# A decoder layer on one core: the fourth blocks of queries and keys as one unit by tokens, and the last eight heads beside w_out

## The chip, the core and the metric

The kernel runs on one core of one Trainium2 chip. The metric is device time in microseconds of one execution of the whole program; the figure given for a kernel is the median of its runs. The engines are named as in the profile: PE (matmuls; its weight loads are listed apart as PEld), DVE (vector), ACT (scalar activations), POOL (GpSimd), and SP, which issues DMAs. PSUM, where matmuls accumulate, has eight banks of 128 x 512 floats.

## What is computed

One layer of a hybrid decoder, all in float32, for 256 tokens of width 2048. In the reference, cut to what matters here:

```python
proj = einsum('bsd,de->bse', rmsnorm(h), w_in)            # z | x,B,C | dt | q | k | v
...                                                        # SSD heads -> y_ssm (256 x 2048)
qh = q.reshape(b, s, 16, 128) * 128 ** -0.5                # 16 heads of 128
for window, dilation in ((128, 1), (512, 4), (2048, 16)):  # three dilated causal windows
    o, l = dilated_window_attention(qh, kh, vh, window, dilation)
y_att = sum of the three outputs, weighted by softmax over their lse
h = h + rmsnorm(concat([y_ssm, y_att]) @ w_out)
h = h + rmsnorm(relu(rmsnorm(h) @ w_up) ** 2 @ w_down)
```

With 256 tokens the three windows become one softmax with a count of how often each key is seen (`m0`, `m1` hold the logarithm of the count). Queries, keys and values have 2048 columns each, in four blocks of 512 columns; a block holds four heads.

## The kernel before

**Precision.** Each float32 operand is split into a high part (`hi`, by ACT, L147) and a rest (`lo`, by DVE, L148), and a product takes three matmuls (hi x hi, hi x lo, lo x hi) at the fast float32 rate. So each weight tile that arrives by DMA costs ACT and DVE one split each, into one of `BUFS = 5` pairs of `hi` and `lo` buffers of 128 x 1024 (two stacked tiles of 128 x 512: one k is 256 rows of the weight).

**Three ways to multiply.** *By features* (`gemm_features`, `products`, L485 and L488): the weight is the stationary operand and the activations stream, so the result has features on the partitions, which is what the scores of attention want. *By tokens* (`row_tile`, L331 to L333): the activations are stationary and 512 weight columns stream; the result has tokens on the partitions. *By seven* (`seven`, L418 to L420): for one k, two blocks of columns and both halves of the tokens, seven products in place of eight, after Strassen and Winograd. It needs sums of activations (`sums_of_acts`, L377 to L383, kept once made), sums of weights on DVE (L252), four pairs of split buffers a group, and the sum of two weight tiles that POOL makes in DRAM by an accumulating DMA (`next_pair`, L279 and L280, four groups ahead); SP then loads it (L156). Its products go to eight banks: four in `acc` and four in `more`, of which two are the small-tile banks (`psmall`, two in all).

**A unit** (`unit`, L451) does two blocks of columns by tokens. It goes through k in a given order, each k plainly (two `row_tiles`, one a block) or by seven; at the first group of seven it calls `drain`, and after the last one `combine` takes `more` away. The last k is always plain and ends the accumulators. `keys_by_tokens` is such a unit for one block of queries with one of keys; since its results have tokens on the partitions, `turned_heads` turns them on PE (L966) and ACT copies them out (L967). `two_values` is such a unit for two blocks of values.

**What runs beside.** Work that isn't a GEMM is written as generators in the queue `waiting`. After each row tile or pair of weight tiles `pump(n)` takes n steps, each time from the generator at the front, which then goes to the back; `drain` runs all to their end. `heads(...)` puts two lanes there, each with two heads at a time: a step of scores and softmax (L907, L908 on PE; L915 to L921 on DVE and ACT), one that turns the probabilities (L929, copies L933), and one that multiplies by the values (L938, L939) and splits the result into `att`, the activations of w_out. The first two steps take both small banks.

**The order around the change.** Blocks are counted from zero. Queries and keys 0 are made by features (`keys_too`), then come the units of queries and keys 1, values 0 and 1, and queries and keys 2. Then:

- queries 3 by features, with pumps (1, 1, 0, 2, 1, 2, 2, 2) for the turns of unit 2 and for heads 0 to 7 (two lanes, twelve steps);
- the values 2 and 3;
- keys 3 by features, with pumps (0, 0, 1, 1, 1, 1, 2, 2) for heads 8 to 11;
- the first `EARLY = 5` k of w_out, for two blocks of columns: ten row tiles (L1278 to L1281), one pump each, for heads 12 to 15.

Then the pools of the attention are closed, and their memory becomes that of `hp`, where w_out keeps, among others, the buffers for sums (`tmp`). w_out goes on with its order (L440): k 5 and 7 plainly, then 6, 9 and 8 by seven, and so on.

**Who orders.** The program's order is a priority, and the scheduler of the language places each engine's instructions at build time; the splits and the sums have a higher priority (`high_priority`), and `in_line` keeps the splits of a unit in a fixed order. Heads and turns are tied behind the last row tile by `issue_after(product[t].ins)`.

Of the kernel before, what the change touches and what calls it, by code (L numbers as in the profile page):

```python
# [10 lines left out]
F32 = mybir.dt.float32  # L11
# [5 lines left out]
P = 128  # L17
S = 256
D = 2048
NT = S // P  # L20
# [15 lines left out]
COL_Q = COL_DT + 32  # L36
COL_K = COL_Q + NH * DH
COL_V = COL_K + NH * DH
NB = 512
# [38 lines left out]
def hymba_layer(ctx: ExitStack, tc: tile.TileContext, x, norm_mix_pre, w_in, conv_w, conv_b, dt_bias, a_log,  # L78
# [53 lines left out]
    def bank():  # L132
        return pacc.tile([P, NB], F32, name="acc")
# [298 lines left out]

    plan("z", w_z, 0, (0, 2, 4, 6, 1, 3, 5), (1, 3))
    plan("z", w_z, 2, (0, 2, 1, 4, 3, 6, 5), (1, 3, 5))
    qk_blocks = [(COL_Q + hb * NB, COL_K + hb * NB) for hb in range(3)]
    plan("qk", w_in, qk_blocks[1], (0, 2, 1, 4, 3, 5, 6), QK_SEVENS)
    plan("v", w_v, 0, range(7), V_SEVENS)
    plan("qk", w_in, qk_blocks[2], (0, 2, 1, 3, 4, 5, 6), QK_SEVENS)
    plan("v", w_v, 2, (0, 2, 1, 3, 4, 5, 6), V_SEVENS)
    plan("out", w_out, 0, (5, 7, 6, 9, 8, 11, 10, 13, 12), (6, 8, 9, 10, 12))  # L440
    plan("out", w_out, 2, (0, 6, 1, 9, 2, 12, 4, 3, 8, 5, 10, 7), (6, 9, 12, 4, 8, 10, 7))
# [7 lines left out]
    plan(("down", 1), w_downs[1], 2, (0, 1, 3, 2, 6, 8, 4, 11, 13, 5, 9, 12), (3, 6, 8, 11, 13, 9, 12))  # L449

    def unit(src, n, order, last, acc, more, combine, lag=0, at_end=(None, None), first=True, ending=None,  # L451
             ready=None, halves=None):


        cols = blocks_of(n)
        sevens = [k for k, by_seven in order if by_seven]
        for i, (k, by_seven) in enumerate(order):
            if i + 1 < len(order) and order[i + 1][1]:
                sums_of_acts(order[i + 1][0])
            if by_seven:  # L460
                if k == sevens[0]:
                    drain()
                    if ready:
                        ready()
                seven(src, *cols, k, acc, more, k == sevens[0], k == sevens[-1])
            else:
                for b in range(2):
                    row_tiles(src, cols[b], [k], acc[b::2], room["acts"], first and i == 0, False,
                              fetch=fetch_next)
            if k == sevens[-1]:  # L470
                combine(more)
        for b in range(2):
            if b and ending:
                ended.append(ending(cols[b], last, acc))
            else:
                row_tiles(src, cols[b], last, acc[b::2], room["acts"], False, True, lag if b else 0, at_end[b],
                          fetch=fetch_last if b else fetch_next, halves=halves if b else None)
# [488 lines left out]
                nc.tensor.transpose(p[:, f * P:(f + 1) * P], r[:, f * P:(f + 1) * P], ident)  # L966
        nc.scalar.activation(dst[:, :, t * P:(t + 1) * P], p.rearrange("p (f s) -> p f s", f=4), AF.Copy)  # L967

    def keys_by_tokens(hb, last, acc, more):

        if hb == 1:
            rstq.append(mp.tile([P, NT], F32, name="rstq"))
# [1 line left out]
        rows, both = [], []  # L974

        def ready():
            rows[:] = [not_yet[1][:, t:t + NT] for t in (0, NT)]
            both.append(mp.tile([P, 4, S], F32, name="cT", bufs=5))
            both.append(mp.tile([P, 4, S], F32, name="cT", bufs=5) if hb == 1 else
# [2 lines left out]
        def end(b):  # L982
            def at_end(t, a):
# [6 lines left out]

        unit(w_in, qk_blocks[hb], orders["qk", qk_blocks[hb]], last, acc, more,
             lambda x: combine_new([[v[:, t] for t in range(NT)] for v in rows], x), 0, (end(0), end(1)),
             ready=ready)
        return both

    rstq = []
# [54 lines left out]
    ap_ = ExitStack()  # L1051
    ap = ap_.enter_context(tc.tile_pool(name="ap", bufs=2, side="right", reuse_waits="tile"))
    heads((0, *qk[0], vs[0]), (1, *qk[1], vs[1]))
    q3 = queries(COL_Q + 3 * NB, rbq, (1, 1, 0, 2, 1, 2, 2, 2))
    own_places([mp.tile([P, 4, S], F32, name="cT", bufs=5).rearrange("p (k f) s -> p k (f s)", k=KB) for _ in range(2)])
    vs += two_values(2, [bank() for _ in range(2 * NT)], [])
    heads((2, *qk[2], vs[2]))
    qk.append((q3, queries(COL_K + 3 * NB, rbc, (0, 0, 1, 1, 1, 1, 2, 2))))
    heads((3, *qk[3], vs[3]))
    del room["own"], room["sum"]  # L1060


# [214 lines left out]
    acc = [bank() for _ in range(2 * NT)]  # L1277
    for k in range(EARLY):  # L1278
        for b in range(2):
            row_tiles(w_out, b * NB, [k], acc[b::2], part, k == 0, False, pumps=1,  # L1280
                      fetch=fetch_next)  # L1281
    assert not waiting
    ap_.close()
# [273 lines left out]
```

## Time and profile before

| | |
|---|---|
| median of 3 runs | 1453.36 us |
| lowest and highest | 1452.56 and 1453.89 us |
| span of the profiled execution, from its first to its last instruction | 1451.4 us |
| median over that span | 1.96 us |
| PE busy | 1442.4 us, 99% |
| DVE busy | 1300.4 us, 90% |
| ACT busy | 947.1 us, 65% |
| granted clock of PE | 0.999 |
| queries 3, from 482.5 us | 30.85 us |
| values 2 and 3, from 513.35 us | 47.76 us |
| keys 3, from 561.11 us | 29.34 us |
| the ten early row tiles of w_out, from 590.45 us | 33.92 us |

The profile is of one execution; times are from the start of its span. The stages in the lower rows were marked by the first matmul of each in PE's order of time. A busy PE need not be at its peak: the duration of a matmul includes its latency, and consecutive ones overlap, so what a matmul costs is read from the distance between starts. A line number is that of the kernel; many instructions carry the line of a helper (L147 and L148 are all splits).

### The profile page before, as it was taken

The numbers are of one execution on the slowest core, as the hardware profiler recorded it, in microseconds if no ns is written. First come the engines' busy times: TensorE is split into PE (matmuls) and PEld (weight loads), VectorE is DVE, ScalarE is ACT, GpSimd is POOL, SyncE is SP. The second block draws the span as 40 slices with busy tenths as digits, with TensorE's granted clock in tenths as the row PEclk, the third lists the DMA queues.
The fourth block names the chain that finished last, engine by engine and source line by source line (L and its number), as shares of the span: only waits on it lengthen the run. The fifth ranks groups of instructions, "written<-read, shape, count | busy, mean of one in ns | idle before, by whom it ended". The sixth has DMA issues, their size and how long they took to land.

```text
span 1451.4 us, 20394 instructions
## 1 busy us (share of the span) xinstructions
PE 1442.4 (99%) x7042; PEld 1214.7 (84%) x7042; DVE 1300.4 (90%) x1881; ACT 947.1 (65%) x1351; POOL 162.3 (11%) x244
## 2 busy tenths in 40 slices
PE   9999999999999999999999999999999999999998
PEld 8888888888888888888888888888888888888886
DVE  7788888988999788689988999999889999999998
ACT  7577669665666666556657677656465776766664
POOL 0201110131111000010100011010111110101000
PEclk9999999999999999999999999999999999999999
DMA  8977656756898658588976798688888888788854
GB/s 267 272 219 222 189 175 187 239 170 195 231 253 248 196 127 244 173 270 257 280 225 217 210 311 240 203 221 251 249 255 279 255 245 247 210 293 265 248 179 160
DMA packets 172359, 332.97 MB, mean 229 GB/s; under 512 B 16048, under 2 KB 18976, under 8 KB 172256
## 3 DMA queue, kind: packets, MB, share of 16 engines
q1 hardware_dynamic: 144736, 272.37, 58.1%
q0 software_dynamic: 19648, 45.63, 15.7%
q10 hardware_dynamic: 7872, 13.68, 2.8%
q8 instruction: 55, 0.90, 0.3%
q14 instruction: 48, 0.39, 0.1%
HBM read 327.39 MB, written 49.84 MB: 260 GB/s over the span
## 4 chain that ended last, share of the span: by engine, by line
PE 76%; ACT 1%; DVE 1%; DMA 0%; issue 0%; ACTq 0%
PE acc L331 10%; PE acc L333 10%; PE acc L332 10%; PE acc L418 7%; PE acc L419 7%; PE acc L420 7%; PE acc L485 4%; PE ps L331 3%; PE ps L332 3%; PE ps L333 3%; PE ps L418 2%; PE ps L419 2%; PE ps L420 2%; PE acc L488 2%; PE acc L1463 1%; PE ps L938 0%
## 5 line engine op out<-in xcount | busy, mean ns | idle before, releaser
L148 DVE TENSOR_TENSOR lo<-raw,hi 128x1024 fp32r<-128x1024 f32 (+1 forms) x387 | 470.1, 1220 | 79.1 <-ACT hi L147 76.3
L147 ACT ACTIVATE hi<-raw 128x1024 fp32r<-128x1024 f32 (+1 forms) x387 | 404.2, 1050 | 204.2 <-PE acc L333 71.4
L485 PE MATMUL acc<-ua,hi 128*128 128x512 f32 x520 | 141.2, 401 | 0.1
L147 ACT ACTIVATE hi<-e 128x1024 fp32r<-128x1024 f32 x66 | 70.2, 1063 | 68.5 <-DVE e L252 62.7
L485 PEld LDWEIGHTS acc<-ua,hi 128*128 128x128 f32 x520 | 91.3, 189 | 14.2 <-ACT hi L147 0.2
L331 PE MATMUL acc<-hi,ua 128*128 128x512 f32 x228 | 90.6, 397 | 0.0
L332 PE MATMUL acc<-lo,ua 128*128 128x512 f32 x228 | 89.3, 392 | 0.0
L333 PE MATMUL acc<-hi,ua 128*128 128x512 f32 x228 | 89.2, 391 | 0.0
L331 PE MATMUL acc<-hi,sh 128*128 128x512 f32 x220 | 86.9, 395 | 0.0
L333 PE MATMUL acc<-hi,sl 128*128 128x512 f32 x220 | 85.8, 390 | 0.0
L332 PE MATMUL acc<-lo,sh 128*128 128x512 f32 x220 | 85.7, 390 | 0.0
L488 PEld LDWEIGHTS acc<-ua,lo 128*128 128x128 f32 x520 | 76.5, 190 | 8.9
L148 DVE TENSOR_TENSOR lo<-e,hi 128x1024 fp32r<-128x1024 f32 x66 | 80.5, 1220 | 0.0
L488 PE MATMUL acc<-ua,lo 128*128 128x256 f32 x520 | 78.8, 282 | 0.0
L419 PE MATMUL acc<-lo,ah 128*128 128x512 f32 x180 | 70.1, 390 | 0.0
L420 PE MATMUL acc<-hi,al 128*128 128x512 f32 x180 | 70.1, 390 | 0.0
L418 PE MATMUL acc<-hi,ah 128*128 128x512 f32 x180 | 70.1, 390 | 0.0
L485 PE MATMUL acc<-uc,hi 128*128 128x512 f32 x208 | 61.4, 405 | 0.0
L148 DVE TENSOR_TENSOR lo<-ha,hi 128x1024 fp32r<-128x1024 f32 x43 | 52.5, 1221 | 6.0 <-ACT hi L147 5.8
L147 ACT ACTIVATE hi<-ha 128x1024 fp32r<-128x1024 f32 x43 | 45.2, 1057 | 19.4 <-PE acc L333 12.4
L147 ACT ACTIVATE hi<-r 128x512 fp32r<-128x512 f32 x66 | 41.5, 629 | 20.8 <-PE acc L333 8.8
L418 PE MATMUL acc<-hi,ua 128*128 128x512 f32 x137 | 53.7, 392 | 0.0
(572 smaller groups left out, 3722.3 us busy)
## 6 DMA issues: line engine op xcount, KB each, us to landing
raw<-in_w_in_dram SPq DMA_DIRECT2D x154, 512.0 KB, 4.5
raw<-in_w_down_dram SPq DMA_DIRECT2D x69, 512.0 KB, 5.7
raw<-in_w_up_dram SPq DMA_DIRECT2D x65, 512.0 KB, 4.8
raw<-in_w_out_dram SPq DMA_DIRECT2D x38, 512.0 KB, 5.1
raw<-pair SPq DMA_DIRECT2D x57, 256.0 KB, 4.3
pair<-in_w_up_dram POOLq DMA_DIRECT2D x56, 256.0 KB, 5.4
pair<-in_w_down_dram POOLq DMA_DIRECT2D x52, 256.0 KB, 6.3
pair<-in_w_in_dram POOLq DMA_DIRECT2D x42, 256.0 KB, 5.5
```

The lines of the kernel that those rows point to most:

```text
L147: return (nc.scalar.activation(hi, src, AF.Copy), nc.vector.tensor_tensor(lo, src, hi.bitcast(F32), op=ALU.subtract))
L148: nc.vector.tensor_tensor(lo, src, hi.bitcast(F32), op=ALU.subtract))
L331: nc.tensor.matmul(dst[:, cs], a_h[:, r, ts], hi[:, j, cs], start=begin and j == 0, stop=False)
L332: nc.tensor.matmul(dst[:, cs], a_h[:, r, ts], lo[:, j, cs], start=False, stop=False)
L333: product[t] = nc.tensor.matmul(dst[:, cs], a_l[:, r, ts], hi[:, j, cs], start=False, stop=end and j == KB - 1)
L418: nc.tensor.matmul(dst, a_h, hi[:, j], start=own and first, stop=False)
L419: nc.tensor.matmul(dst, a_h, lo[:, j], start=False, stop=False)
L420: nc.tensor.matmul(dst, a_l, hi[:, j], start=False, stop=own and last)
L485: nc.tensor.matmul(acc[f], hi[:, j, f * P:(f + 1) * P], u(k0 + j), start=k0 + j == 0, stop=False, skip_group_check=True)
L488: nc.tensor.matmul(acc[f][:, 0], lo[:, j, f * P:(f + 1) * P], u(k0 + j)[:, 0], start=False, stop=k0 + j == NK - 1, skip_group_check=True)
L1463: nc.tensor.transpose(p[:, f * P:(f + 1) * P], r[:, f * P:(f + 1) * P], ident)
```

## The change

Queries 3 and keys 3 are no longer two GEMMs by features but one unit by tokens (`keys_by_tokens(3, ...)`), with the order of k (0, 2, 4, 1, 3, 5, 6, then 7) and three groups of seven, 3, 5 and 6 (the third unit has four). It stands where queries 3 stood, ahead of the values; its plain row tiles pump (2, 2, 1, 1, 1, 1, 2, 2) steps for the turns of unit 2 and heads 0 to 7, and what is left is drained at its first group of seven. Its results go to two `tk` buffers and, turned on PE beside the values' first row tiles, to two `cT` buffers. The values take the unit's `more` as accumulators and its accumulators as their `more`. Heads 8 to 15 are now one queue of two lanes with twelve steps, and all of it runs beside w_out's ten early row tiles, which pump one step for the first block of columns and, from the second k on, two for the second.

```diff
-    qk_blocks = [(COL_Q + hb * NB, COL_K + hb * NB) for hb in range(3)]
+    qk_blocks = [(COL_Q + hb * NB, COL_K + hb * NB) for hb in range(4)]
...
     plan("qk", w_in, qk_blocks[2], (0, 2, 1, 3, 4, 5, 6), QK_SEVENS)
+    plan("qk", w_in, qk_blocks[3], (0, 2, 4, 1, 3, 5, 6), (3, 5, 6))
     plan("v", w_v, 2, (0, 2, 1, 3, 4, 5, 6), V_SEVENS)
...
     def unit(src, n, order, last, acc, more, combine, lag=0, at_end=(None, None), first=True, ending=None,
-             ready=None, halves=None):
+             ready=None, halves=None, pumps=(1,)):
...
+        turns = 0
...
                     row_tiles(src, cols[b], [k], acc[b::2], room["acts"], first and i == 0, False,
-                              fetch=fetch_next)
+                              pumps=pumps[turns % len(pumps)], fetch=fetch_next)
+                    turns += 1
...
-    def keys_by_tokens(hb, last, acc, more):
+    def keys_by_tokens(hb, last, acc, more, pumps=(1,)):
...
         def ready():
+            if hb == 3:
+                rows[:] = [mp.tile([P, NT, NB], F32, name="tk", bufs=3) for _ in range(2)]
+                both.extend(mp.tile([P, 4, S], F32, name="cT", bufs=5) for _ in range(2))
+                more.extend(f() for f in (psmall, bank, psmall, bank))
+                return
...
-             ready=ready)
+             ready=ready, pumps=pumps)
...
     heads((0, *qk[0], vs[0]), (1, *qk[1], vs[1]))
-    q3 = queries(COL_Q + 3 * NB, rbq, (1, 1, 0, 2, 1, 2, 2, 2))
+    acc, more = [bank() for _ in range(2 * NT)], []
     own_places([mp.tile([P, 4, S], F32, name="cT", bufs=5).rearrange("p (k f) s -> p k (f s)", k=KB) for _ in range(2)])
-    vs += two_values(2, [bank() for _ in range(2 * NT)], [])
-    heads((2, *qk[2], vs[2]))
-    qk.append((q3, queries(COL_K + 3 * NB, rbc, (0, 0, 1, 1, 1, 1, 2, 2))))
-    heads((3, *qk[3], vs[3]))
+    qk.append(keys_by_tokens(3, (7,), acc, more, (2, 2, 1, 1, 1, 1, 2, 2)))
+    vs += two_values(2, more, acc)
+    heads((2, *qk[2], vs[2]), (3, *qk[3], vs[3]))
...
     for k in range(EARLY):
         for b in range(2):
-            row_tiles(w_out, b * NB, [k], acc[b::2], part, k == 0, False, pumps=1,
+            row_tiles(w_out, b * NB, [k], acc[b::2], part, k == 0, False, pumps=1 + (k > 0 and b),
                       fetch=fetch_next)
```

## The prediction

> **What bounds the kernel now.** I read the page first, then who waited for whom on PE, and then the stretch that the change rebuilds, by windows. From the page, and from the list of PE's waits over the whole span (total, times, longest, in us):
>
> ```profile
> span 1451.4 us, 20394 instructions
> PE 1442.4 (99%) x7042; PEld 1214.7 (84%) x7042; DVE 1300.4 (90%) x1881; ACT 947.1 (65%) x1351; POOL 162.3 (11%) x244
> PE ps L1408 <- ACT dg L1407: 1.4, 1, 1.4
> PE ps L810 <- ACT bn L816: 0.6, 1, 0.6
> ```
>
> PE is busy 99% of the span, and its waits of any length are in the warm-up, in the SSD part (L810) and at the end (L1408); none lies in attention. So time is PE's own work: a microsecond of matmuls taken away is one won, and the only loss can be a wait that PE doesn't have now. The stretch in question, by stage (columns: from:to, length, busy of PE, PEld, DVE, ACT, POOL with counts, clock, DMA share, GB/s): the unit of the third query and key blocks, then q3 (with heads 0 to 7), the values, k3 (with heads 8 to 11) and the first ten tiles of w_out (with heads 12 to 15):
>
> ```profile
> 441.70:482.50 40.80, 40.80 (x181) 33.80 (x180) 38.14 (x45) 26.36 (x29) 4.87 (x7) 1.00 0.76 213
> 482.50:513.35 30.85, 30.85 (x190) 27.22 (x188) 20.91 (x46) 19.75 (x40) 1.90 (x3) 1.00 0.71 204
> 513.35:561.11 47.76, 47.76 (x227) 39.82 (x226) 41.77 (x73) 27.97 (x46) 3.52 (x5) 1.00 0.63 170
> 561.11:590.45 29.34, 29.33 (x174) 25.78 (x173) 20.61 (x45) 20.08 (x39) 0.00 (x0) 1.00 0.66 209
> 590.45:624.37 33.92, 33.92 (x166) 28.48 (x165) 23.09 (x54) 19.28 (x36) 1.35 (x2) 1.00 0.66 218
> ```
>
> PE is busy throughout at clock 1.00. DVE has room in q3, k3 and w_out's tiles (68% to 70%) and little in a unit by tokens (38.14 of 40.80, 93%).
>
> **The parts, on PE.** Removed: q3 and k3 by features, eight pairs of 128-row weight tiles each. PE's order of time in k3 (start, duration):
>
> ```profile
> 563.89 1.99 PE L485 MATMUL acc<-ua,hi 128*128 128x512 f32 x8
> 565.71 1.11 PE L488 MATMUL acc<-ua,lo 128*128 128x256 f32 x8
> 566.67 2.00 PE L485 MATMUL acc<-ua,hi 128*128 128x512 f32 x8
> ```
>
> From one start to the next (durations overlap, since matmuls are pipelined) a pair takes 566.67 - 563.89 = 2.78 us. 16 pairs are 44.5 us. Added: a unit by tokens. The values show its two kinds of step:
>
> ```profile
> 540.71 0.39 PE L331 MATMUL acc<-hi,ua 128*128 128x512 f32 x1
> 546.15 0.39 PE L418 MATMUL ps<-hi,ub 128*128 128x512 f32 x1
> 555.67 0.39 PE L331 MATMUL acc<-hi,uc 128*128 128x512 f32 x1
> ```
>
> Plain: 24 matmuls from 540.71 to 546.15, 5.44 us for one k and both columns blocks, 2.72 a row tile. By seven: 42 matmuls from 546.15 to 555.67 are two groups, 4.76 each, so a group saves 0.68. Eight k with three groups cost 8 x 5.44 - 3 x 0.68 = 41.5 us. The row of 441.70 agrees: the same unit with four groups took 40.80 = 41.5 - 0.68.
>
> Added too: 16 transposes of L966, in four groups, because a unit by tokens leaves q and k with tokens on the partitions. One such group inside q3, and its durations over the whole kernel (min/median/max ns):
>
> ```profile
> 485.30 0.60 PE L966 MATMUL acc<-ident,al 128*128 128x128 f32 x4
> 485.66 2.11 PE L485 MATMUL acc<-ua,hi 128*128 128x512 f32 x8
> 488.55 0.60 PE L966 MATMUL ps<-ident,al 128*128 128x128 f32 x4
> L966 PE MATMUL acc<-ident,al x16: 270/272/273, 401.8 to 495.3; 128*128 128x128 f32 x16
> ```
>
> The four hold the stream for 0.36 us, and the pair behind them takes 488.55 - 485.66 = 2.89 instead of 2.78: 0.46 a group, 1.84 for four. Sum of the terms: -44.5 + 41.5 + 1.84 = **-1.2 us**.
>
> The trace's 272 ns is a latency, not a hold of PE. [...]
>
> The heads' matmuls are the same, at other places. Price in w_out's tiles: 33.92 - 10 x 2.72 = 6.72 us for two lanes (two heads each), 3.36 a lane. A second sum, by stages at that price: new unit 41.5 + 1.84 (transposes of the third blocks, which q3 had) + 4 x 3.36 = 56.8; values 40.8 + 1.84 = 42.6; ten tiles 27.2 + 4 x 3.36 = 40.6; together 140.0 against 30.85 + 47.76 + 29.34 + 33.92 = 141.87: **-1.8 us**. The two differ by what breaking into a feature stream costs beyond breaking into a token stream, which no row separates. I take -1.5 and keep -1.2 and -1.8.
>
> **Costed at nothing.** DVE in the new unit: from the 441.70 row, a group fewer saves three adds (L252, 0.69), one split of 1.22 and one of 0.69, 4.0 together, so 34.1; four lanes add some 3.7 each (softmax from 499.74 to 502.72, 3.0, and a split of 0.68; these rows stand below), so 48.9 of PE's 56.8 us, 86%: hidden behind PE on average. The values have 38.1 of 42.6. POOL and DMA: three more pairs of accumulating copies ahead of the values' and w_out's own (four groups ahead), and fewer SP loads of 512 KB whole. One unit with four groups has POOL at 4.87 of 40.80 and DMA at 0.76 and no PE wait; three groups in 56.8 us ask less. If a pair came late, one wait of a landing, some 5 us, would show. What ACT and DVE did at the ends of q3 and k3 (L508, L509, L949) goes; the unit's combine and ends (L427 to L431, L986, L987) are what the third unit has already.
>
> **What can turn into a wait: two places.** First, w_out. Its first group of seven needs sums of activations, which need buffers in memory that the last heads give back:
>
> ```profile
> 612.26 0.59 PE L938 MATMUL ps<-pT,tk 128*128 128x256 f32 x2
> 613.49 0.48 PE L331 MATMUL acc<-hi,sh 128*128 128x512 f32 x1
> 613.60 1.23 DVE L148 TENSOR_TENSOR lo<-raw,hi 128x1024 fp32r<-128x1024 f32 x1 [2.25 <-ACT hi L147]
> 614.74 0.68 DVE L377 TENSOR_TENSOR r<-sh,sl 128x512 f32<-128x512 f32 x1
> 615.35 0.68 DVE L148 TENSOR_TENSOR al<-ps,ah 128x512 fp32r<-128x512 f32 x1
> 615.95 0.41 DVE L378 TENSOR_TENSOR r<-r 128x256 f32<-128x256 f32 x1
> 616.88 0.28 DVE L379 TENSOR_TENSOR r<-r 128x128 f32<-128x128 f32 x1
> 617.41 0.29 DVE L380 TENSOR_TENSOR r<-r 128x128 f32<-128x128 f32 x1
> 634.18 0.69 DVE L252 TENSOR_TENSOR e<-raw 128x512 f32<-128x512 f32 x1
> 647.89 1.22 DVE L148 TENSOR_TENSOR lo<-uc,hi 128x1024 fp32r<-128x1024 f32 x1
> 649.89 0.39 PE L332 MATMUL acc<-lo,ah 128*128 128x512 f32 x1
> 622.00:635.40 13.40, 13.40 (x61) 11.09 (x60) 10.68 (x17) 7.39 (x9) 1.90 (x3) 1.00 0.93 304
> 635.40:640.00 4.60, 4.60 (x22) 3.82 (x21) 3.94 (x6) 3.48 (x4) 0.00 (x0) 1.00 0.67 143
> 650.00:666.00 16.00, 16.00 (x73) 13.24 (x72) 16.00 (x24) 10.19 (x12) 2.17 (x3) 1.00 0.89 255
> ```
>
> DVE idled 2.25 us and began the sums (L377) right after the last head's products, which ran from 612.26 to 613.49. From there it works up to the tile that PE reads at 649.89, whose split ended at 647.89 + 1.22 = 649.11: 0.8 us of lead, the least I found; from 650 on DVE is busy 16.00 of 16.00. Now the last head follows the sixth of ten tiles; with pumps of 1, 1, 1, 2, 1, 2, ... twelve steps end behind the ninth, 3 x 2.72 = 8.2 us later against PE. By then the five split buffers (BUFS) can be full, so DVE's splits aren't late; the sums are. What is left to do at that point grows by about 3.5 us: the sums of group 6 (0.68 + 0.41 + 0.28 + 0.29 and a split of 0.68: 2.4) and all but the split of those of group 9 (1.7), one split of heads (0.7), less one split done earlier (1.2). DVE's idle time from 622 to 640 is 18.0 - 10.68 - 3.94 = 3.4 us. 3.4 + 0.8 covers 3.5, with nothing over: on time costs 0, and each microsecond that the heads end later costs about one.
>
> Second, the new unit's first group of seven drains the lanes at once: four steps with no tile between them. A lane's step takes both small PSUM banks, so they go one by one. From the heads of q3 and, for the transposes, of the values:
>
> ```profile
> 498.26 0.39 PE L907 MATMUL ps<-cT 128*128 128x128 f32 x2
> 499.74 0.28 DVE L915 CUSTOM_DVE_ANT_0 sm<-ps,cst 128x128 f32<-128x128 f32 x1
> 500.85 0.08 DVE L915 DVE_READ_ACCUMULATOR2_ANT mx<- 128x1 f32 x1
> 502.17 0.55 DVE L921 TENSOR_SCALAR sm<-sm,den 128x128 f32<-128x128 f32 x2
> 525.03 0.82 PE L929 MATMUL ps<-ident,sm 128*128 128x128 f32 x6
> 507.48 0.84 ACT L933 ACTIVATE pT<-ps 128x384 f32<-128x384 f32 x2
> 510.05 0.60 ACT L147 ACTIVATE ah<-ps 128x512 fp32r<-128x512 f32 x1 [0.97 <-PE ps L939]
> ```
>
> Scores until the banks are read: 498.26 to 500.93, 2.7 us, twice; transposes 0.6 (six, their durations overlapping) and copies 0.84, twice; two products of 613.49 - 612.26 = 1.23; split 0.60 + 0.68: 12 us, of which PE works some 6 (scores 1.2, transposes 0.6 and products 1.2, each twice). The other 6 must be filled. Of a group's 21 matmuls 15 need no small bank (3.4 us), and five buffers let two groups run so far, 6.8 us: just filled, if the order on PE puts them there. I take 0.5 us for both places together, from 0 and the two prices below.
>
> **Sum.** -1.5 + 0.5 = -1.0 us: the span would be 1450.4. The median shown is 1453.36, 1.96 over this span, and I keep that difference: **1452.4 us**. A measurement of this kernel tells 0.2% (2.9 us) from no change, so this is no change.
>
> **Rivals.**
> (A) The forecast: from -1.8 with no wait to about +0.5. 66%.
> (B) Slower: the heads end later than behind the ninth tile, since the fourth steps of the two lanes now come in one pump, each wants both small banks, and only one tile (2.72) follows until the first lane's fifth. If they need two tiles more, DVE's lead is 5.4 us short and PE waits at the second and third groups of seven: -1.5 + 5.4 = +3.9, 1457.3. Slower than before from 1.5 us of lateness, by more than 0.2% from 4.4. For it: 0.8 us of lead. Against: tiles further on can go ahead of a waiting head. 13%.
> (C) Slower: nothing fills the drain in the new unit, and 6 us of wait stand between its fourth k and its first group: -1.5 + 6 = +4.5, 1457.9. For it: PE takes matmuls as they are ordered. Against: the values drain too, and their PE is busy 47.76 of 47.76, though only one step is left there. 10%. [...]
> (D) Faster: the steps that are pumped in twos save some six breaks of 0.24 us beside the -1.8: -3.2, 1450.2. The L966 rows show 0.11 a break behind transposes; I doubt more. 7%.
> (E) A transpose holds PE for its whole duration, 16 x 0.272 = 4.4 instead of 1.84: -1.2 + 2.5 = +1.3, 1454.7; no gain from the change. Against: starts 0.36 us apart for four. 4%.
>
> **Range and chances.** (A) and (E) lie within 0.2%, with a little of (A) on the fast side; most of (D) is faster; half of (B) and nearly all of (C) slower. Faster 0.08, within 0.76, slower 0.16. From 1450.2 (D) to 1457.3 (the middle of B); outside are (C), half of (B) and the end of (D), under 0.2. (A) alone: 1451.6 to 1453.9.
>
> **What would show it.** L485 and L488 lose 256 starts in attention and L966 has 48 records, not 32; the stretch from the third unit's end to w_out's eleventh tile is 140 us instead of 141.87; PE's waits name neither L418 nor L331 there. (B) is wrong if L377 starts soon after the ninth tile and no wait for DVE shows at w_out's groups; (C) if the first L418 of the new unit follows without idling. I am wrong if the stretch shrinks by over 3 us, or if a wait shows in stages that the change doesn't touch.

## The result and the profile after

The changed kernel takes **1460.36 us** (median of 4 runs, 1459.92 to 1463.94) against 1452.96 us of the kernel before beside it (1452.37 to 1453.89): a ratio of 1.0055, 95% interval 1.0043 to 1.0068. Two later series of five runs each gave 1461.76 (1.0057, 1.0045 to 1.0070) and 1460.70 us (1.0051, 1.0037 to 1.0065). So it is slower by some 8 us, where 1 us less was forecast, and 3.1 us outside the range.

Line numbers of the changed kernel are a little higher than before: scores L910 and L911 (before L907, L908), the reading of the scores on DVE L918 (L915), the turned probabilities L932 (L929), the products with the values L941 and L942, the turns L969 (L966), the ends of a unit of queries and keys L994, those of the values L1019 and L1020. L331 to L333, L418 to L420, L147, L148 and L161 have kept theirs.

The page of the changed kernel, span and PE:

```profile
span 1462.2 us, 20325 instructions
...
PE 1446.7 (99%) x6985; PEld 1213.3 (83%) x6985; DVE 1308.6 (89%) x1892; ACT 952.8 (65%) x1358; POOL 166.9 (11%) x250
```

The profiled execution (1463.94 us) is the slowest of the four; why it is slower than the others is settled below. Its span is 10.8 us longer than the one before, and PE is counted busy 4.3 us longer, so two fifths of the loss is not idle time. The list of PE's waits over the whole span (total, times, longest, in us) names what is new:

```profile
PE ps L910 <- DVE mx L918: 4.8, 1, 4.8
PE ps L332 <- DVE lo L148: 1.5, 1, 1.5
...
PE acc L418 <- ACT hi L147: 0.5, 1, 0.5
PE acc L419 <- DVE lo L148: 0.2, 1, 0.2
```

None of the four stands in the list before. By windows (from:to, length, busy of PE, PEld, DVE, ACT, POOL with counts, clock, DMA share, GB/s), the same stretch of the span, from the end of the third unit to w_out's eleventh row tile:

```profile
482.50:513.00 30.50, 30.50 (x159) 25.79 (x158) 21.50 (x47) 17.97 (x37) 3.32 (x5) 1.00 0.73 198
513.00:536.10 23.10, 22.34 (x110) 17.57 (x109) 18.00 (x44) 16.50 (x34) 0.81 (x1) 1.00 0.35 83
536.10:586.20 50.10, 48.64 (x222) 39.68 (x221) 43.96 (x53) 29.74 (x35) 5.43 (x8) 1.00 0.81 227
586.20:592.80 6.60, 6.60 (x33) 5.52 (x31) 4.62 (x6) 3.20 (x4) 0.00 (x0) 1.00 0.93 331
592.80:597.90 5.10, 0.35 (x2) 0.00 (x0) 3.21 (x8) 3.60 (x7) 0.00 (x0) 0.93 0.94 284
597.90:604.90 7.00, 6.97 (x20) 5.71 (x21) 5.34 (x25) 4.45 (x17) 0.00 (x0) 0.56 0.73 251
604.90:635.50 30.60, 30.60 (x159) 25.33 (x157) 16.91 (x42) 16.62 (x35) 2.71 (x4) 1.00 0.50 137
```

The rows are the unit's first plain tiles, its groups of seven with the drain, its end with the values, and four pieces of w_out's ten early tiles. From its first matmul, at 482.81, the stretch is 152.6 us long; it was 142.0. From its start to w_out's first matmul it takes 103.4, and w_out's ten tiles take 49.2 us. Two rows stand out: 592.80 to 597.90, where PE does nothing, and the 7 us behind it, where PE is busy but its clock is 0.56. That second row is where busy PE time is lost without a wait.

**What PE waits for at 592.8.** PE's order of time there:

```profile
592.77 0.39 PE L333 MATMUL acc<-hi,sl 128*128 128x512 f32 x1
597.93 0.79 PE L910 MATMUL ps<-tk,cT 128*128 128x128 f32 x2 [4.78 <-DVE mx L918]
...
600.30 0.99 PE L331 MATMUL acc<-hi,sh 128*128 128x512 f32 x1
601.08 0.63 PE L332 MATMUL acc<-lo,sh 128*128 128x512 f32 x1
```

The two lanes of heads 8 to 15 start beside w_out: lane A's scores stand behind w_out's first tile, lane B's behind its second, both on PE in an order that is fixed when the program is built. Lane B's scores need the two small banks, which hold lane A's scores until L918 has read them. DVE's order of time says why it hadn't:

```profile
590.48 2.50 DVE L148 TENSOR_TENSOR lo<-raw,hi 128x1024 fp32r<-128x1024 f32 x2 [1.94 <-ACT hi L147]
593.92 1.23 DVE L148 TENSOR_TENSOR lo<-raw,hi 128x1024 fp32r<-128x1024 f32 x1 [0.94 <-ACT hi L147]
596.10 1.23 DVE L148 TENSOR_TENSOR lo<-raw,hi 128x1024 fp32r<-128x1024 f32 x1 [0.94 <-ACT hi L147]
597.24 0.28 DVE L918 CUSTOM_DVE_ANT_0 sm<-ps,cst 128x128 f32<-128x128 f32 x1
```

Lane A's scores are done at about 590, but four splits for later tiles stand ahead of L918 on DVE, and DVE idles between them: it is not short of time but stuck behind an instruction whose input isn't there. ACT makes that input, and ACT in turn waits for weights:

```profile
589.39 1.06 ACT L147 ACTIVATE hi<-raw 128x1024 fp32r<-128x1024 f32 x1 [5.38 <-DMA raw<-in_w_out_dram]
590.66 1.06 ACT L147 ACTIVATE hi<-raw 128x1024 fp32r<-128x1024 f32 x1 [0.21 <-DMA raw<-in_w_out_dram]
```

The gap before the third and that before the fourth split (0.94 each) have another source: ACT made those two `hi` without waiting, each behind 1.3 us of the values' ends (L1020) in its own order. The loads behind the late splits, issued from 579 to 584 us (KB each, median us to landing), took 9.1 us:

```profile
raw<-in_w_out_dram SPq DMA_DIRECT2D x3, 512.0 KB, 9.1
pair<-in_w_out_dram POOLq DMA_DIRECT2D x1, 256.0 KB, 9.1
```

The second row is one of POOL's accumulating copies for w_out's sums of weights. It is issued at 579.52, just ahead of the three loads, and takes as long as they do; the two loads of w_out before it took 4.5 us in the median. With keys 3 by features, no such copy is issued from 565 to 600 us: the copies are made four groups of seven ahead, and the values, which have the last groups before w_out's, lie earlier there. That the copy slows the loads is not shown, since no run takes it away.

PE itself had no use for those four splits yet: the weights of the third tile, which PE reads from 600.30 on, were split at 591.7. A chain for tiles that were not due held up one that was: loads, ACT, DVE's order, the small banks, PE's order.

### The profile page after: what moved, and what is told of

Read it like the earlier page. It is cut to its first block, busy times and chain, and to the rows that moved or that the text cites. A ratio compares the mean times of both kernels' runs of the same rounds, so it can differ in the third digit from the quotient of the medians.

```text
span 1462.2 us, 20325 instructions
## 1 busy us (share of the span) xinstructions
PE 1446.7 (99%) x6985; PEld 1213.3 (83%) x6985; DVE 1308.6 (89%) x1892; ACT 952.8 (65%) x1358; POOL 166.9 (11%) x250
## 4 chain that ended last, share of the span: by engine, by line
PE 71%; DVE 3%; DMA 2%; ACT 1%; issue 0%; SPq 0%; DVEq 0%; ACTq 0%
PE acc L331 10%; PE acc L333 10%; PE acc L332 10%; PE acc L419 6%; PE acc L420 6%; PE acc L418 6%; PE ps L331 3%; PE ps L333 3%; PE ps L332 3%; PE ps L418 2%; PE ps L420 2%; PE ps L419 2%; PE acc L488 2%; DVE lo L148 2%; PE acc L491 1%; DMA raw<-in_w_in_dram 1%
## 5 line engine op out<-in xcount | busy, mean ns | idle before, releaser
L147 ACT ACTIVATE hi<-raw 128x1024 fp32r<-128x1024 f32 (+1 forms) x387 | 403.7, 1050 | 199.5 <-PE acc L333 63.2
L148 DVE TENSOR_TENSOR lo<-raw,hi 128x1024 fp32r<-128x1024 f32 (+1 forms) x387 | 469.2, 1218 | 68.9 <-ACT hi L147 65.8
L488 PE MATMUL acc<-ua,hi 128*128 128x512 f32 x440 | 119.5, 400 | 0.0
L147 ACT ACTIVATE hi<-e 128x1024 fp32r<-128x1024 f32 x66 | 70.1, 1063 | 70.9 <-DVE e L252 66.9
L331 PE MATMUL acc<-hi,ua 128*128 128x512 f32 x248 | 98.7, 399 | 0.0
L333 PE MATMUL acc<-hi,ua 128*128 128x512 f32 x248 | 96.9, 391 | 0.0
L332 PE MATMUL acc<-lo,ua 128*128 128x512 f32 x248 | 96.8, 390 | 0.0
L331 PE MATMUL acc<-hi,sh 128*128 128x512 f32 x220 | 88.3, 401 | 0.0
L488 PEld LDWEIGHTS acc<-ua,hi 128*128 128x128 f32 x440 | 77.1, 189 | 11.7
L333 PE MATMUL acc<-hi,sl 128*128 128x512 f32 x220 | 86.2, 392 | 0.0
L148 DVE TENSOR_TENSOR lo<-e,hi 128x1024 fp32r<-128x1024 f32 x66 | 80.4, 1218 | 0.0
L419 PE MATMUL acc<-lo,ah 128*128 128x512 f32 x193 | 75.4, 391 | 0.2 <-DVE lo L148 0.2
L418 PE MATMUL acc<-hi,ah 128*128 128x512 f32 x193 | 75.1, 391 | 0.5 <-ACT hi L147 0.5
L420 PE MATMUL acc<-hi,al 128*128 128x512 f32 x193 | 75.3, 390 | 0.0
L491 PEld LDWEIGHTS acc<-ua,lo 128*128 128x128 f32 x440 | 64.8, 189 | 7.6
L491 PE MATMUL acc<-ua,lo 128*128 128x256 f32 x440 | 66.7, 281 | 0.0
L148 DVE TENSOR_TENSOR lo<-ha,hi 128x1024 fp32r<-128x1024 f32 x43 | 52.4, 1220 | 6.1 <-ACT hi L147 5.7
L147 ACT ACTIVATE hi<-ha 128x1024 fp32r<-128x1024 f32 x43 | 45.2, 1057 | 19.2 <-PE acc L333 10.9
L333 PEld LDWEIGHTS acc<-hi,ua 128*128 128x128 f32 x248 | 46.6, 188 | 9.9
L331 PEld LDWEIGHTS acc<-hi,ua 128*128 128x128 f32 x248 | 46.6, 188 | 9.4 <-ACT ua L149 0.3
L332 PEld LDWEIGHTS acc<-lo,ua 128*128 128x128 f32 x248 | 46.6, 188 | 9.1
```

Source lines behind the costliest of these rows:

```text
L147: return (nc.scalar.activation(hi, src, AF.Copy), nc.vector.tensor_tensor(lo, src, hi.bitcast(F32), op=ALU.subtract))
L148: nc.vector.tensor_tensor(lo, src, hi.bitcast(F32), op=ALU.subtract))
L331: nc.tensor.matmul(dst[:, cs], a_h[:, r, ts], hi[:, j, cs], start=begin and j == 0, stop=False)
L332: nc.tensor.matmul(dst[:, cs], a_h[:, r, ts], lo[:, j, cs], start=False, stop=False)
L333: product[t] = nc.tensor.matmul(dst[:, cs], a_l[:, r, ts], hi[:, j, cs], start=False, stop=end and j == KB - 1)
L418: nc.tensor.matmul(dst, a_h, hi[:, j], start=own and first, stop=False)
```

## The experiments

All are edits of the changed kernel, but for the third, which edits the one before. Where a stage is given in us, it goes from start to start on PE in the profiled execution, and the stretch begins with the first matmul of queries 3 or of the new unit.

**1. The heads start a k later** (w_out's first two tiles pump nothing, then 1 and 2):

```diff
-            row_tiles(..., pumps=1 + (k > 0 and b),
+            row_tiles(..., pumps=k > 0 and 1 + b,
```

> The changed kernel took 1460.4 us; its profile has a PE wait of 4.8 us where lane B's first scores of heads 8 to 15 stand behind w_out's second tile. This kernel pumps no step during w_out's first k (two tiles) and then 1, 2, 1, 2, ... steps, twelve in eight tiles. Theory 1 (head of line): the wait is there because the splits and loads for w_out's first tiles have no lead at that moment, so lane A's first softmax stands on DVE behind splits that wait for loads; two tiles later the loads have caught up: the wait is gone or under 1 us, and the time is 1455 to 1456.5. Theory 2 (twelve steps beside ten tiles are too many wherever they begin): the steps are packed closer, so the time is 1459 to 1463, and the last heads end later, with a wait of DVE at w_out's groups of seven.

Measured: 1458.62 us (1456.34 to 1459.26), ratio 1.0035 (1.0022 to 1.0048), between the two. The wait at lane B's scores is 1.8 us, another of 0.6 stands at L932, and w_out's ten tiles take 43.6 us. Starting later shortens the wait and does not remove it, since lane A's softmax still stands behind splits.

**2. Lane A's softmax ahead of the splits on DVE.** The last reading of lane A's scores is put into the fixed order of the splits, so that those of later tiles come behind it:

```diff
+    reads = []
...
-                nc.vector.tensor_tensor_reduce(sm[:, cs], s[:, cs], mk, ...)
+                reads.append(nc.vector.tensor_tensor_reduce(sm[:, cs], s[:, cs], mk, ...))
...
+                if (hb, j) == (2, 2):
+                    line["dve"] = reads[-1]
                 yield from attention(ap, 4 * hb + j, ...)
```

The edge is set as lane B begins with heads 10 and 11, when the last reading recorded is lane A's.

> The changed kernel with one edge of order on DVE: the splits that follow w_out's second tile come behind lane A's first softmax reads instead of ahead of them. PE's work, the loads and the pumps stay. Theory 1: the 4.8 us wait of lane B's first scores goes, since the reads are done as soon as lane A's scores are: 1455 to 1456.5. If instead PE lacks weights there (loads as such are too late), a wait for a split at the third or fourth tile takes its place: 1459 to 1461.

Measured: 1457.46 us (1456.97 to 1457.72), ratio 1.0031 (1.0020 to 1.0043). DVE in this kernel (L920 is the reading of the scores there):

```profile
589.69 0.29 DVE L920 CUSTOM_DVE_ANT_0 sm<-ps,cst 128x128 f32<-128x128 f32 x1 [2.68 <-PE ps L913]
...
590.91 4.63 DVE L148 TENSOR_TENSOR lo<-raw,hi 128x1024 fp32r<-128x1024 f32 x4
```

The reading now waits for PE alone, and the four splits run behind it in one piece. The wait of 4.8 us is gone and the clock stays at 1.00; w_out's ten tiles take 42.5 us instead of 49.2. So without that order on DVE there is no such wait. The time is 1 us above what T1 expected: small waits are left in w_out's tiles (0.3 and 0.3 at the turned probabilities), and the drain's.

**3. The late heads alone.** The kernel before, with queries 3 and keys 3 still by features, but heads 8 to 15 as one queue beside w_out:

```diff
-    heads((2, *qk[2], vs[2]))
-    qk.append((q3, queries(COL_K + 3 * NB, rbc, (0, 0, 1, 1, 1, 1, 2, 2))))
-    heads((3, *qk[3], vs[3]))
+    qk.append((q3, queries(COL_K + 3 * NB, rbc, (0,))))
+    heads((2, *qk[2], vs[2]), (3, *qk[3], vs[3]))
...
-            row_tiles(w_out, ..., pumps=1,
+            row_tiles(w_out, ..., pumps=1 + (k > 0 and b),
```

> The kernel before, queries 3 and keys 3 by features, but heads 8 to 15 all beside w_out's ten tiles with the pumps of the change (nothing is pumped beside keys 3). Theory 1: keys 3 by features leave DVE and the loads far ahead when w_out begins, so the first steps find no queue on DVE: 1452 to 1454, no PE wait over 1 us in w_out. Theory 2 (as the prediction's rival B: the heads end too late and DVE lacks the time for the sums): 1455 to 1458, with PE waits at w_out's second and third groups of seven.

Measured: 1453.51 us (1453.09 to 1453.78), ratio 1.0004 (0.9994 to 1.0013): 0.65 us more in the medians, which the interval doesn't tell from nothing, and no wait of PE is listed from 480 to 700 us. Twelve steps beside ten tiles cost next to nothing by themselves, and so does ending behind the ninth. By windows, up to w_out and its ten tiles:

```profile
482.50:583.40 100.90, 100.90 (x542) 86.65 (x541) 76.72 (x133) 61.91 (x103) 5.43 (x8) 1.00 0.68 198
583.40:624.70 41.30, 41.30 (x211) 34.35 (x210) 26.81 (x77) 24.01 (x55) 2.73 (x4) 1.00 0.59 177
```

The same two lanes stand beside the same ten tiles in 41.3 us here and in 49.2 in the changed kernel. What differs is what goes before. SP's issues of w_out's weights, in this kernel and then in the changed one (start, time from the first issue to the last, count):

```profile
566.70 15.84 SPq L161 DMA_DIRECT2D raw<-in_w_out_dram  x8
```

```profile
576.21 11.53 SPq L161 DMA_DIRECT2D raw<-in_w_out_dram  x6
```

With a GEMM by features ahead of w_out, the first of its weights is asked for 16.7 us before w_out's first matmul (583.37), and those issued from 570 to 577 us landed in 5.1 us:

```profile
raw<-in_w_out_dram SPq DMA_DIRECT2D x4, 512.0 KB, 5.1
```

With the values ahead of it, it is asked for 10.0 us before (586.19), and w_out's second tile has its split 3.1 us before PE reads it, where the late heads alone had 11.1. A unit by tokens leaves less lead than keys 3 by features did.

**4. No steps left to drain in the new unit.** Sixteen steps are handed out behind its eight first plain tiles:

```diff
-    qk.append(keys_by_tokens(3, (7,), acc, more, (2, 2, 1, 1, 1, 1, 2, 2)))
+    qk.append(keys_by_tokens(3, (7,), acc, more, (2,)))
```

> The changed kernel, but the unit of queries and keys 3 pumps two steps after each of its eight plain tiles, sixteen in all, so that its first group of seven drains nothing. Wait of 4.8 us in w_out untouched. If the drain is what costs the unit its gain (about 1.9 us of gaps between 513 and 536 us in the changed kernel's profile, and through the late DVE another wait of 1.5 us at the values' first tile): 1457 to 1458.5. If three groups of seven in a row are what makes DVE late there, the 1.5 us stay: 1458.5 to 1459.5. If neither, 1460 to 1461.

Measured: 1458.62 us (1454.80 to 1462.25), ratio 1.0034 (1.0023 to 1.0045). Up to w_out's first matmul it takes 100.88 us instead of 103.38, and all three waits of the unit and the values are gone; PE's one wait from 480 to 640 us is the known one:

```profile
PE ps L910 <- DVE mx L918: 3.6, 1, 3.6
```

So the drain costs 2.5 us here, 2.2 of it in waits. In the changed kernel these are two at the groups of seven and one at the values' first tile, where DVE, late from the drained lanes and the groups, comes with the split just behind the unit's ends:

```profile
522.89 0.50 PE L419 MATMUL acc<-lo,ah 128*128 128x512 f32 x1 [0.23 <-DVE lo L148]
...
531.57 0.50 PE L418 MATMUL acc<-hi,ah 128*128 128x512 f32 x1 [0.51 <-ACT hi L147]
...
544.18 0.50 PE L332 MATMUL ps<-lo,ua 128*128 128x512 f32 x1 [1.46 <-DVE lo L148]
```

```profile
542.31 0.69 DVE L994 TENSOR_TENSOR tk<-acc,tk 128x512 f32<-128x512 f32 x1 [0.44 <-PE acc L333]
542.91 1.22 DVE L148 TENSOR_TENSOR lo<-raw,hi 128x1024 fp32r<-128x1024 f32 x1
```

**5. Both repairs** (2 and 4 together).

> The changed kernel with both repairs at once: on DVE the softmax of lane A's heads stands ahead of the splits of w_out's tiles, and the new unit hands out all its sixteen head steps behind its plain tiles, so that none are left to drain. T1 (two separate costs, the drain some 3 us and the wait in w_out's tiles with its slow clock some 7): the savings add; the stretch from the third unit's end to w_out's eleventh tile is 100.65 + 42.5 = 143.2 us, no wait of PE over 0.7 us stands in it, and the time is 1453 to 1455. T2 (the two costs are one: the lanes are late whichever place shows it): a wait of 1 to 3 us shows at a third place, and the time stays at 1456.5 to 1458.5.

Measured: 1456.04 us (1454.63 to 1458.31), ratio 1.0021 (1.0013 to 1.0030). The profiled run took 1455.21, its stretch 101.11 + 43.17 = 144.28 us, against 100.88 + 42.52 = 143.40 by the two repairs' own runs (the 100.65 of the expectation starts 0.23 us into the unit). The savings nearly add, and a new wait takes some of it (L934: the turned probabilities, which need the small banks too):

```profile
PE ps L934 <- DVE mx L920: 1.4, 1, 1.4
```

The median is between the two theories, so this alone decides nothing; what is left is the banks again.

**6. Four loads taken away.** w_out's k = 1 and 2 take the raw weights of the tile before:

```diff
+        if room.get("again") is not None:
+            return room["again"]
...
-            return fetch(src, k0, c0, into=into, pair=pair)
+            room["last"] = fetch(src, k0, c0, into=into, pair=pair)
+            return room["last"]
...
     for k in range(EARLY):
         for b in range(2):
+            room["again"] = room["last"] if 0 < k < 3 else None
```

> The changed kernel, in which w_out's second and third row tiles (k = 1 and 2, four tiles of weights) are not loaded: they take the raw weights that the tile before has in its buffer, so those two k of w_out are computed with other weights, and four loads of 512 KB are left out. The orders of DVE and PE stay. T1 (loads: the softmax on DVE stands behind splits that wait for weights which land 8.6 to 9.2 us after their issue): without those landings the four splits run early, the wait of 4.8 us at lane B's scores shrinks below 1 us, the granted clock stays at 1.00, and the time is 1455 to 1457. T2 (DVE itself: it is behind with its own work, and landings only happen to coincide): the wait stays above 3 us, and the time stays at 1459 to 1461.

Measured: 1456.34 us (1455.47 to 1457.75), ratio 1.0024 (1.0014 to 1.0034). DVE (L921 reads the scores):

```profile
587.91 4.63 DVE L148 TENSOR_TENSOR lo<-raw,hi 128x1024 fp32r<-128x1024 f32 x4
592.45 0.29 DVE L921 CUSTOM_DVE_ANT_0 sm<-ps,cst 128x128 f32<-128x128 f32 x1
```

The same four splits still stand ahead of the reading, but they end at 592.5 instead of 597.2, and PE doesn't wait at lane B's scores at all; w_out's ten tiles take 41.4 us, what they take with the late heads alone. So the wait needs both: splits ahead of the softmax, and weights that land late for them.

**7. Order, drain and loads together** (2, 4 and 6).

> The kernel with both repairs (lane A's softmax ahead of the splits on DVE, no steps left to drain), and w_out's k = 1 and 2 not loaded but computed with the raw weights of the tile before, so that four loads of 512 KB are left out. It is to show what the new unit is worth when nothing waits. T1 (the unit by tokens gains 0.2 us over the features once waits are gone, and the late heads cost 0.2): no wait of PE over 0.3 us from 482 to 700 us, w_out's ten tiles in 41.3 to 42.0 us, and the time within 1 us of the kernel before, 1452.2 to 1453.7. T2 (the lanes and the tiles get in each other's way on PE even without waits): no wait, and still 1454 to 1456.

Measured: 1453.64 us (1452.98 to 1454.73), ratio 1.0006 (0.9997 to 1.0015), as T1 has it. PE's waits from 480 to 700 us:

```profile
PE acc L422 <- DVE lo L148: 0.3, 1, 0.3
```

w_out's ten tiles take 41.3 us. Once nothing waits, the rebuilt stage costs what the old one did (143.2 us from start to end against 142.0, with 1.0 us between the times, too little to tell): no gain is hidden under the waits.

**8. Four groups of seven** (5, with k = 1 by seven as well):

```diff
-    plan("qk", w_in, qk_blocks[3], (0, 2, 4, 1, 3, 5, 6), (3, 5, 6))
+    plan("qk", w_in, qk_blocks[3], (0, 2, 4, 1, 3, 5, 6), (1, 3, 5, 6))
...
-    qk.append(keys_by_tokens(3, (7,), acc, more, (2,)))
+    qk.append(keys_by_tokens(3, (7,), acc, more, (2, 2, 3, 3, 3, 3)))
```

> The kernel with both repairs, with four groups of seven in the new unit in place of three (k 1, 3, 5 and 6), its sixteen head steps handed out behind six plain tiles. T1 (PE's own work sets the time, and DVE holds the splits and sums beside the lanes): one group more saves 0.68 us on PE: 0.5 to 0.8 us below the kernel with three groups and both repairs. T2 (DVE has no room for a fourth group beside four lanes, or the lanes drain again): waits of PE at the unit's groups of seven or at the values' first tile, and 1 to 4 us above it.

Measured: 1458.57 us (1458.16 to 1461.72), ratio 1.0044 (1.0032 to 1.0057), 2.5 us above the kernel with three groups and both repairs. T2:

```profile
PE ps L332 <- DVE lo L148: 1.5, 1, 1.5
PE acc L418 <- ACT hi L147: 1.4, 2, 0.9
```

The same waits as the drain's are back, with no step to drain: PE meets ACT and DVE with four lanes and a unit's splits and sums at once. That one group more or a few drained steps are enough to tip it is read from these waits; what is scarce, DVE's time or its order, no run separates.

**9. Matmuls in the wait.** Sixteen matmuls of 128x256 that nothing reads, ahead of lane B's scores; the later of two kernels has eight:

```diff
         with tc.issue_after(product[0].ins), tc.issue_after(product[1].ins):
+            if h == 10:
+                q = bank()
+                for _ in range(16):
+                    nc.tensor.matmul(q[:, 0:2 * P], qT[:, 0, P:], kT[:, 0], start=True, stop=True)
```

> The changed kernel with sixteen matmuls of 128x256 put on PE between w_out's second tile and the scores of lane B's heads; they repeat a product of lane A's scores into a spare bank, and nothing reads them. At the 218 ns that L911 takes from one start to the next they fill 3.5 of the 4.8 us in which PE stood idle; beside them one split moves ahead of lane B's softmax on DVE. T1 (the clock falls because PE idles): PE is busy up to about 1 us before lane B's scores, the granted clock stays at 1.00 from 597 to 605 us where it was 0.50 to 0.60, and the tiles behind take 2.7 us in place of 4.7: the ten tiles of w_out take 45 to 46.5 us instead of 49.2, and the time is 1456 to 1458.5 though PE has 3.5 us more to do. T2 (the clock falls for another reason at this place, the transfers or the burst of work behind the wait): the clock is 0.5 to 0.6 as before, and the time is 1460 or more.

Measured: 1462.51 us (1462.13 to 1462.67), ratio 1.0067 (1.0054 to 1.0080). The expectation had the size wrong: a matmul of this form has two records of 218 ns, so sixteen took 6.9 us, longer than any wait. So the time falls into T2's range, and the clock is T1's. PE:

```profile
592.75 7.07 PE L911 MATMUL acc<-tk,cT 128*128 128x256 f32 x32
599.65 0.38 PE L914 MATMUL ps<-tk,cT 128*128 128x128 f32 x2
```

The clock stayed at 1.00, and w_out's ten tiles took 48.2 us: 41.3 and the 6.9 of the filler. They were still 1 us shorter than with 4.8 us of idling in the changed kernel's profile. The kernel with eight, with the changed one beside it:

> The changed kernel with eight instead of sixteen matmuls of 128x256 ahead of lane B's scores; each has two records of 218 ns, so eight take 3.5 us of the 3 to 5 us that PE waits, and add nothing to it where the wait is longer. T1 (the clock falls because PE idles for long): less than 1.5 us of idle time is left, the granted clock stays at 1.00 up to 605 us, w_out's ten tiles take 41.3 + 3.5 to 5 = 44.8 to 46.3 us, and the time is 1457.5 to 1459.5, some 3 us under the changed kernel's usual 1460 to 1462. T2 (the clock falls for another reason there): clock 0.5 to 0.6 for some us and 1460 to 1462.5.

> The changed kernel beside it on the same chip: 1460 to 1462 in most executions, with a wait of 3 to 5 us and the slow clock, and 1457 to 1458 in one where the wait is under 2 us.

Measured: **1459.15 us** (1458.87 to 1460.83) with the eight matmuls and **1460.70** (1459.51 to 1461.30) without on the same chip. PE and the clock with them:

```profile
592.41 3.61 PE L911 MATMUL acc<-tk,cT 128*128 128x256 f32 x16
...
595.86 0.38 PE L914 MATMUL ps<-tk,cT 128*128 128x128 f32 x2
```

```profile
592.80:597.90 5.10, 5.10 (x27) 4.47 (x27) 3.91 (x13) 3.58 (x10) 0.00 (x0) 1.00 0.97 301
597.90:604.90 7.00, 7.00 (x38) 5.69 (x36) 4.97 (x20) 4.88 (x13) 0.00 (x0) 1.00 0.51 178
```

Without them the wait was 3.0 us, and the clock fell behind it:

```profile
PE ps L910 <- DVE mx L918: 3.0, 1, 3.0
```

```profile
592.80:596.80 4.00, 1.04 (x6) 0.70 (x5) 2.90 (x11) 2.50 (x7) 0.00 (x0) 1.00 0.76 249
596.80:602.00 5.20, 5.20 (x19) 4.16 (x19) 4.64 (x21) 3.69 (x13) 0.00 (x0) 0.67 0.92 330
```

With useless work on PE the median is 1.55 us lower; the ranges overlap, so the times alone are no proof. The profiles are plainer: w_out's ten tiles take 44.7 us with it, 41.3 and 3.45 of filler, and 46.1 without, 41.3 + 3.0 of wait + 1.8 of slow clock. So in these two executions the slow clock goes with PE's idling, and not with the work behind the wait, which is the same program in both, or with the transfers: the DMA share is 0.97 in the row with the filler, where the clock is 1.00, and 0.92 in the one with 0.67. The gain is half of the 3 us expected, because the wait in this execution was 3.0 and not 4.8.

**10. The changed kernel again** in a series of its own.

> The changed kernel once more, on the chip that runs the two beside it, for a narrower interval and its spread: 1459.5 to 1464, median 1460 to 1461, if the wait in w_out's tiles with the slow clock behind it is in every run.

Measured: 1457.64, 1461.55, 1461.76, 1461.84 and 1462.36 us. The first, which is below the range expected, is the profiled one, and it tells the spread:

```profile
PE ps L910 <- DVE mx L918: 1.5, 1, 1.5
```

```profile
587.18 1.06 ACT L147 ACTIVATE hi<-raw 128x1024 fp32r<-128x1024 f32 x1 [1.42 <-DMA raw<-in_w_out_dram]
```

```profile
592.80:597.90 5.10, 3.59 (x18) 3.00 (x18) 4.91 (x21) 3.74 (x14) 0.00 (x0) 1.00 0.99 322
```

In this execution the three loads issued from 578 to 584.5 us landed in 6.0 us in the median (the copy beside them in 7.1) instead of 9.1, ACT waited 1.4 us for the late ones instead of 5.4, PE 1.5 instead of 4.8, the clock never fell, and the ten tiles took 43.05 us instead of 49.21. The difference of 6.2 us is that of the two times, 1463.94 - 1457.64 = 6.3. The kernel before has no such wait, and its runs lie within 2.2 us of each other (1452.05 to 1454.27).

## Why the prediction was wrong, point by point

In the profiled executions the stretch grew by 10.6 us (and the span by 10.8). By the stages of the late heads alone (100.89 + 41.31 = 142.20), of no drain (100.88 up to w_out) and of the changed kernel (103.38 + 49.21 = 152.59), it divides so:

| | us | as predicted |
|---|---|---|
| heads 8 to 15 beside w_out, by themselves | +0.2 | the same matmuls elsewhere, 0 |
| the unit by tokens in place of the features, nothing drained | 0.0 | -1.2 to -1.8 |
| the drain in the unit, with its waits | +2.5 | 0.5, with the next |
| w_out's ten tiles: the wait at lane B's scores, 4.8 | +4.8 | in the 0.5 above, at the end of the heads |
| the slow clock behind it | +3.1 | not in the sum |
| together | +10.6 | -1.0 |

This execution is the slowest. In one near the median (1460.70 us, in experiment 9) the wait is 3.0 us and the slow clock costs 1.8, the stretch is 103.32 + 46.10 = 149.42 us long and so 7.4 longer than before, and the medians are 7.8 us apart. The second and third rows are good to about 1 us: the two later kernels without a drain took 101.11 (experiment 5) and 101.90 us (experiment 7) where the fourth took 100.88.

**"The parts, on PE": the starts went as counted, and the gain came to nothing.** Of the starts, 256 of L485 and L488 are gone from the stretch, and the turns have 32 records there instead of 16. They cost 1.5 us more, against 1.84 taken. The failed term is what a stream loses to the work put into it. From start to start, the features of the late heads alone take 45.7 us where sixteen undisturbed pairs make 44.5; the plain tiles and groups of seven which the unit adds take 43.8 (52.25 + 33.70 - 22.84 - 19.28) where 41.5 was worked out from undisturbed ones; the heads take 0.4 more. So 43.8 + 1.5 + 0.4 - 45.7 = 0.0. I had weighed the two sums against each other by what a break costs in a feature stream beyond one in a token stream, and gave the token stream the better of it; here the unit lost 2.3 us to what stands between its tiles and the features 1.2. Which part of the 2.3 is breaks and which is a tile that starts late for its weights, the starts don't separate. Rival (D) falls with it, and rival (E) too: 16 turns at 272 ns would be 4.4 us, and they took 1.5.

**"Costed at nothing" failed, and most of the loss is there (7.9 of the 10.6 us, the wait and the slow clock behind it).** It compared DVE's work with PE's time as an average over a stage: 48.9 of 56.8 us in the unit, with POOL and DMA asked for less. DVE was idle for part of the 5 us in which PE waited for it (busy 3.21 of 5.10). What counted was the order on DVE, and what the split at its front waited for. And it held that fewer and whole loads are no risk. Of the moved step I counted instructions and not lead: keys 3 by features was also the time in which SP, ACT and DVE got w_out's weights ready, 16.7 us ahead of w_out against 10.0 now. The values now stand there, with DVE at 43.96 of 50.10 us together with the unit's end. For POOL it asked whether a pair would come late, and not whether the copies would now stand beside w_out's first loads, as one does.

**"Two places" named two; one was the wrong one.** At w_out I looked for the end of the heads, rival (B): its sums late after the last head, 5.4 us. No wait of PE for them is listed, and the late heads alone, with the same pumps, cost 0.2 us in the stretch. So (B) is rejected; the wait came at the start of the same heads, which I had gone past. The question "each wants both small banks" stood in (B), applied to the fourth steps; it decided at the first.

Second, the drain, rival (C): right in place, and its price too high. I had 6 us if nothing filled it; it costs 2.5, and no wait for a step of the lanes is listed there. What was left is splits: L418 waits for ACT and L419 for DVE, and two thirds of the waiting comes some 12 us later, at the values' first tile. "Just filled" for 0.5 us was too kind: it counted PE's matmuls and left out that DVE must bring their weights while it serves four lanes.

**The clock.** The sum has no term for it: the windows of the prediction all have 1.00. The runs show one. It was 0.56 in the mean over the 7 us behind a wait of 4.8 us, 0.67 over the 5.2 us behind one of 3.0, and 1.00 behind those of 1.5 and 1.8 us (experiments 10 and 1). The slow stretch itself was at 0.50. With the wait of 4.8 us it lasted 6.8 us (597.19 to 604.02) and began 0.7 us before PE's wait ended; with that of 3.0 it lasted 3.4 (597.40 to 600.81) and began 1.3 us after the wait had ended, at 596.07; with the 3.6 of experiment 4 it lasted 3.4 too (0.66 over 594 to 597, 0.54 over 597 to 598.5). What decides between the two lengths isn't shown. With the eight matmuls in the wait of experiment 9 the clock stayed at 1.00. The slow clock cost 1.8 to 3.1 us in these executions, at w_out's tiles and not at the drain.

**What would show it** did its work: L418 and L419 are among PE's waits, and the stretch is 152.6 and not 140. The forecast fell on both signs.

**What stays open.** Why the same loads land in 6 us in one execution and in 9 in another isn't shown. In the profiled executions of the changed kernel they go with the copy of POOL beside them (loads 9.1, 7.8 and 6.0 us, copy 9.1, 7.7 and 7.1); in the third the copy is issued behind two of the three loads and not ahead of them. Which of the two holds up the other, no run tells. And the kernel with order, drain and loads repaired is not a way to a better kernel: it leaves loads out, and is at best even with the one before.

## What to carry to other kernels

When a stage with slack is replaced by one that is as long and has none, ask what the slack was preparing: look when the next stage's first loads are issued, what other transfers stand beside them, and how far its splits are ahead, before and after. On engines with a fixed order, an average of busy time says nothing of a wait; follow, for each scarce buffer (here two small banks), which instruction gives it back, and what stands ahead of that instruction and may be waiting for a DMA. And look at the clock behind a wait of PE too: here waits of 3.0, 3.6 and 4.8 us cost half to two thirds more than their length by it (1.8 us on 3.0, 1.8 on the 3.6 of experiment 4, where w_out's tiles took 46.7 us, and 3.1 on 4.8), and those of 1.5 and 1.8 us, with the clock at 1.00, did not.

## What was not expected of the hardware

That sixteen matmuls without use, 6.9 us of them, leave w_out's tiles done 1 us earlier than 4.8 us of idling (48.2 against 49.2 us, though the whole kernel is no faster for it: 1462.51 against 1461.76 us of the changed one beside it), and that with eight of them the median is 1.55 us lower. That the time of one program moves by over 4 us from execution to execution (1457.64 to 1462.36): in its three profiled ones (1457.64, 1460.70 and 1463.94 us) with the landing of a few loads, since 1.5 us of waiting left the clock at 1.00, and behind 3.0 and 4.8 us it was 0.67 and 0.56 in the mean.
